# Attention turns of a decoder layer: query transposes moved beside the probability transposes

## The chip, the cores and the metric

The kernel runs on one core of one Trainium2 chip. The metric is the device time of one execution in microseconds (us); the number given for a kernel is the median of its runs. Five engines work side by side, each through its own queue in order: PE (TensorE, matrix products and transposes, with its weight loads shown as PEld), DVE (VectorE), ACT (ScalarE), POOL (GpSimd) and SP (SyncE, which issues the DMAs).

## The reference

One layer of a hybrid decoder over 512 tokens and 1024 features, in fp32:

```
h = RMSNorm(x)
[x_rnn | g_rnn | q | k | v | gate_a | gate_b] = h @ w_in
A = (RG-LRU(conv4(x_rnn)) * gelu(g_rnn)) @ w_rnn_proj
B = attention(q, k, v) @ w_attn_proj
x += (sigmoid(gate_a) * A + sigmoid(gate_b) * B) @ w_out
x += relu(RMSNorm(x) @ w_up)^2 @ w_down
x += (p @ w_ple_proj) * sigmoid(RMSNorm(x) @ w_ple_gate)
```

Attention: 16 query heads and 4 key heads of 64, each query head normalised and rotated (rotary embedding), a sliding window of 128 tokens, and a sink per head that joins the softmax's maximum and its sum. The query block of 128 tokens sees its own block of keys and the one before; the first block sees its own alone.

## The kernel before, in words

Weights come in 143 units of 128x1024. Each is loaded, and split by ACT (`wh`, L118) and DVE (`wl`, L119) into two parts, so that a product is three fp32r matmuls (L145 to L147). PE works through the layer: k and v, then q (L258), attention mixed with the products for `gate_b` and `gate_a` ("gates"), the recurrent branch, the output product, the MLP and the last gate.

The attention stage is the loop at L601: eight turns, u = 0 to 7, where turn u handles query block n = u mod 4 for eight of the heads (u < 4 the first eight). A turn has two halves, g = 0 and 1, of four heads each. A half computes the scores on PE (`scores`, tile `S`, one PSUM buffer), masks and copies them and takes the maximum (`softmax_max`: for n > 0 ACT copies to `sm`, L456, DVE merges the other block under a mask, L457, reduces, L464, and makes four small 128x4 tiles, L465 to L468; for n = 0 DVE alone, L459), takes exponentials on ACT (`softmax_exp`, four at L474 and one at L477), and divides by the sum (`softmax_norm`: DVE L482 and L483, then four POOL operations, L486; in the last half of turn 7 DVE does those four). The probabilities are transposed on PE (`p_transpose`, tile `ppt`, L494) and go out of PSUM on DVE twice, each under a mask (`p_evac`, L505; for n = 0 once on ACT, L503). `pv` (L516, tile `po`) multiplies them with v, and `o_split` (L524 on ACT, L525 on DVE) stores the result. Each half also contains one gate product of 24 matmuls (`proj` on p0 or p1), with its evacuation on DVE (`gate_evac`, L596).

The transposes of half 1 of turn u-1 stand in turn u, behind p0 and ahead of the scores of half 1; those of half 0 stand at the end of their own turn. Queries of the next turn are prepared inside a turn: `q_rope` (four DVE operations, L405 to L408, from `q_raw` to the tile `ra`), `q_transpose` (four PE transposes, L417, tile `pqt`; two ACT copies, L423, and two DVE subtractions, L425, to the tiles `qt`), and, two turns ahead, `q_scale` (ACT L386, DVE L388 and L390, POOL L392).

The order of PE, ACT, SP and POOL is the order of the program text (`manual_schedule`, L68). DVE's order is not: a scheduler sets it when the program is built, by its own costs, and it is fixed from then on. A DVE instruction that waits therefore holds whatever the scheduler has put behind it. PSUM: `ppt` and `pqt` share two `tr` buffers, `pgate` and `po` four `mm` buffers; `qt` has four buffers, two turns' worth.

Of the kernel before, what the change touches and what calls it, by code (L numbers as in the profile page):

```python
# [9 lines left out]
F32 = mybir.dt.float32  # L10
F32R = mybir.dt.float32r
AF = mybir.ActivationFunctionType
ALU = mybir.AluOpType
# [57 lines left out]
def layer_kernel(ctx, tc, w_all, x_t, p_t, vecs, row, ctab, out_t):  # L71
    nc = tc.nc
# [32 lines left out]
    def wissue(parts=1):  # L105
        u = order.pop(0)
        ready[u] = wsplit(u, wp, W_BUFS, parts)
# [15 lines left out]
    def wload(u):  # L123

        while u not in ready or (order and len(ready) <= AHEAD):
            wissue()
        return ready.pop(u)
# [110 lines left out]
    def s_ps(name):  # L238
        return ps.tile([P, 4, 256], F32, tag="S", name=name, bufs=1)

    def s_banks(name):
        wide = s_ps(name).rearrange("p a b -> p (a b)")
        return [wide[:, 0:S], wide[:, S : 2 * S]]
# [151 lines left out]
    def q_rope(u):  # L395
        n = u % NB
        src = q_raw.pop(u).rearrange("p (h d) -> p h d", d=HD)
        a = ftile(f"ra_{u}").rearrange("p (h d) -> p h d", d=HD)
        b = ftile(f"rb_{u}").rearrange("p (h d) -> p h d", d=HD)
        tt = nc.vector.tensor_tensor  # L400

        def tb(t, lo, hi):
            return t[:, n, lo:hi].unsqueeze(1).broadcast_to([P, 8, hi - lo])

        tt(out=a, in0=src, in1=tb(ccq, 0, HD), op=ALU.mult)  # L405
        tt(out=b[:, :, 0:32], in0=src[:, :, 32:64], in1=tb(ssq, 0, 32), op=ALU.mult)
        tt(out=b[:, :, 32:64], in0=src[:, :, 0:32], in1=tb(ssq, 32, 64), op=ALU.mult)
        tt(out=a, in0=a, in1=b, op=ALU.add)  # L408
        q_rot[u] = a

    def q_transpose(u, pt=None):


        a = q_rot.pop(u)
        pt = tr_ps(f"pqt{u}") if pt is None else pt
        for i in range(4):
            nc.tensor.transpose(pt[:, i * P : (i + 1) * P],  # L417
                                a[:, 2 * i : 2 * i + 2, :].rearrange("p a d -> p (a d)"), ident)
        qt = [att.tile([P, 4, P], F32R, tag="qt", name=f"qt{u}{j}", bufs=4) for j in range(2)]
        rows = [slice(0, HD), slice(HD, P)]  # L420
        src = [pt[own].rearrange("p (i t) -> p i t", t=P) for own in rows]
        for j, own in enumerate(rows):
            nc.scalar.activation(qt[j][own], src[j], AF.Copy)  # L423
        for j, own in enumerate(rows):
            nc.vector.tensor_tensor(out=qt[j][rows[1 - j]], in0=src[j],  # L425
                                    in1=qt[j][own].bitcast(F32), op=ALU.subtract)
        q_t[u] = qt

    def window(u):
        n = u % NB  # L430
        return max(n - 1, 0), (2 if n else 1)
# [39 lines left out]
    def softmax_exp(u, g):  # L471
        sm, st = probs[u, g]
        for i in range(4):
            nc.scalar.activation(sm[:, i, :], sm[:, i, :], AF.Exp, bias=st[:, 1, i : i + 1],  # L474
                                 scale=q_sc[u][:, 4 * g + i : 4 * g + i + 1],
                                 accum_out=st[:, 2, i : i + 1])
        nc.scalar.activation(st[:, 3], st[:, 3], AF.Exp)  # L477
# [19 lines left out]
    def p_evac(u, g):  # L497
        pt = p_t_.pop((u, g))
        n = window(u)[1]
        for kb in range(n):  # L500
            prt = ftile(f"pt{u}{g}{kb}")
            if n == 1:
                nc.scalar.activation(prt, pt, AF.Copy)  # L503
            else:
                nc.vector.tensor_tensor(out=prt.rearrange("p (i t) -> p i t", t=P),  # L505
                                        in0=pt.rearrange("p (i t) -> p i t", t=P),
                                        in1=heads4(keep[kb]), op=ALU.mult)
            p_t_[u, g, kb] = prt
# [67 lines left out]
    def q_first():  # L576
# [5 lines left out]
    qkv_group(2, q_banks, [  # L582
        lambda: (k_transpose(norm["rot"]), q_first()),
        k_double,
        lambda: q_transpose(0, s_banks("pqt0")[0]),
    ])
    rb = norm["x"]
    q_evac(1, q_banks)
# [10 lines left out]
    fills = [U_GB + m for m in range(KC)] + [U_GA + m for m in range(KC)]  # L599

    for u in range(8):  # L601
        w0 = wload(fills[len(gates)])
        p0 = mm_ps(f"pgate_{u}_0")
        s0 = scores(u, 0)
        softmax_max(u, 0, s0)
        proj(p0, w0, xg)
        if u:
            p_transpose(u - 1, 1)
            p_evac(u - 1, 1)
        softmax_exp(u, 0)  # L610
        if u < 7:
            q_rope(u + 1)
        softmax_norm(u, 0)
        if u < 6:
            q_scale(u + 2)
        gate_evac(p0, f"gate_{u}_0")
        s1 = scores(u, 1)
        if u:
            o_split(u - 1, pv(u - 1))
        softmax_max(u, 1, s1)  # L620
        w1 = ready.pop(fills[len(gates)])
        p1 = mm_ps(f"pgate_{u}_1")
        proj(p1, w1, xg, range(0, CUT))
        if u < 7:
            q_transpose(u + 1)
        wissue()
        softmax_exp(u, 1)
        softmax_norm(u, 1)
        proj(p1, w1, xg, range(CUT, KC))
        gate_evac(p1, f"gate_{u}_1")  # L630
        p_transpose(u, 0)
        p_evac(u, 0)
# [347 lines left out]
```

## Time and profile before

| | us |
|---|---|
| median of 3 runs (lowest, highest) | 837.55 (837.51, 838.27) |
| the profiled execution | 837.6 |
| its span, first to last instruction | 835.5 |
| PE busy in the span | 829.4 (99%) |
| DVE, ACT, POOL busy | 522.1 (62%), 365.0 (44%), 101.4 (12%) |
| attention stage, turns 1 to 7 (first scores of turn 1 to the first matmul of the recurrent branch) | about 87 to 200 |

The profile is one execution; about 2.1 us of its 837.6 lie outside the span. A row of a timeline gives start, duration, engine, line, operation, tiles written and read, shape and count; several equal neighbours are merged into one row, with the time from the first's start to the last's end. In brackets stands the idle time of the engine before the row and what ended it. PE starts a matmul before the one ahead of it has ended, so the distance between starts is its price, not the duration; DVE and ACT overlap neighbours by about 0.1 us.

### The profile page before, as it was taken

The numbers are of one execution on the slowest core, as the hardware profiler recorded it, in microseconds if no ns is written. First come the engines' busy times: TensorE is split into PE (matmuls) and PEld (weight loads), VectorE is DVE, ScalarE is ACT, GpSimd is POOL, SyncE is SP. The second block draws the span as 40 slices with busy tenths as digits, with TensorE's granted clock in tenths as the row PEclk, the third lists the DMA queues.
The fourth block names the chain that finished last, engine by engine and source line by source line (L and its number), as shares of the span: only waits on it lengthen the run. The fifth ranks groups of instructions, "written<-read, shape, count | busy, mean of one in ns | idle before, by whom it ended". The sixth has DMA issues, their size and how long they took to land.

```text
span 835.5 us, 9915 instructions
## 1 busy us (share of the span) xinstructions
PE 829.4 (99%) x3780; PEld 678.9 (81%) x3780; DVE 522.1 (62%) x768; ACT 365.0 (44%) x581; POOL 101.4 (12%) x123
## 2 busy tenths in 40 slices
PE   9999999999999999999999999999999999999997
PEld 7888877877888888888888888888888888888886
DVE  4687798886766878486567533653355435655563
ACT  7434665663578895633343221231222212333430
POOL 2922432421011110000210000000000000012100
PEclk9999999999999999999999999999999999999999
DMA  7344122122232232235333322223223232233141
GB/s 251 126 115 138 51 80 72 51 77 76 76 100 76 76 102 100 76 127 186 131 103 109 104 98 102 89 89 119 86 97 100 101 102 76 100 102 101 51 163 39
DMA packets 25744, 84.00 MB, mean 101 GB/s; under 512 B 3040, under 2 KB 3424, under 8 KB 25696
## 3 DMA queue, kind: packets, MB, share of 16 engines
q1 hardware_dynamic: 25552, 83.32, 30.0%
q8 instruction: 30, 0.49, 0.2%
q14 instruction: 18, 0.15, 0.1%
q10 hardware_dynamic: 144, 0.05, 0.0%
HBM read 80.20 MB, written 2.10 MB: 99 GB/s over the span
## 4 chain that ended last, share of the span: by engine, by line
PE 99%; DMA 0%; DVE 0%; ACT 0%; issue 0%
PE pu L145 7%; PE pd L145 7%; PE pd L147 7%; PE pu L147 7%; PE pd L146 7%; PE pu L146 7%; PE pq L258 5%; PE pgate L145 4%; PE pgate L147 4%; PE pgate L146 4%; PE pkv L258 3%; PE pyb L145 2%; PE S L441 2%; PE px L145 2%; PE pgl L145 2%; PE pyb L146 2%
## 5 line engine op out<-in xcount | busy, mean ns | idle before, releaser
L119 DVE TENSOR_TENSOR wl<-wr,wh 128x1024 fp32r<-128x1024 f32 (+1 forms) x144 | 180.6, 1257 | 56.1 <-ACT wh L118 56.1
L118 ACT ACTIVATE wh<-wr 128x1024 fp32r<-128x1024 f32 (+1 forms) x144 | 149.7, 1045 | 130.5 <-PE pd L146 98.5
L146 PE MATMUL pu<-x1g,wh 128*128 128x512 f32 x256 | 99.6, 389 | 0.0
L145 PE MATMUL pu<-x1g,wh 128*128 128x512 f32 x256 | 99.6, 389 | 0.0
L147 PE MATMUL pu<-x1g,wl 128*128 128x512 f32 x256 | 99.6, 389 | 0.0
L145 PE MATMUL pd<-u,wh 128*128 128x512 f32 x256 | 99.6, 389 | 0.0
L146 PE MATMUL pd<-u,wh 128*128 128x512 f32 x256 | 99.6, 389 | 0.0
L147 PE MATMUL pd<-u,wl 128*128 128x512 f32 x256 | 99.6, 389 | 0.0
L131 ACT ACTIVATE u<-up 128x512 fp32r<-128x512 f32 x32 | 20.2, 633 | 124.4 <-DVE up L847 124.4
L213 POOL TENSOR_TENSOR sq<-sq,sq_x 128x512 f32<-128x512 f32 x14 | 18.2, 1298 | 453.5 <-ACT sq_x L211 453.5
L856 DVE TENSOR_TENSOR xr<-pd,xr 128x512 f32<-128x512 f32 x32 | 22.1, 692 | 81.5 <-PE pd L147 81.5
L147 PEld LDWEIGHTS pu<-x1g,wl 128*128 128x128 f32 x256 | 48.0, 188 | 10.1
L147 PEld LDWEIGHTS pd<-u,wl 128*128 128x128 f32 x256 | 48.0, 188 | 10.0
L146 PEld LDWEIGHTS pd<-u,wh 128*128 128x128 f32 x256 | 48.0, 188 | 10.0
L146 PEld LDWEIGHTS pu<-x1g,wh 128*128 128x128 f32 x256 | 48.1, 188 | 10.0
L145 PEld LDWEIGHTS pd<-u,wh 128*128 128x128 f32 x256 | 48.0, 188 | 9.9
L145 PEld LDWEIGHTS pu<-x1g,wh 128*128 128x128 f32 x256 | 48.0, 188 | 9.9
L145 PE MATMUL pgate<-xg,wh 128*128 128x512 f32 x128 | 51.4, 402 | 0.0
L147 PE MATMUL pgate<-xg,wl 128*128 128x512 f32 x128 | 50.2, 392 | 0.0
L146 PE MATMUL pgate<-xg,wh 128*128 128x512 f32 x128 | 50.0, 391 | 0.0
L846 DVE TENSOR_TENSOR up<-pu,rb_x 128x512 f32<-128x512 f32 x32 | 22.0, 691 | 40.2 <-PE pu L147 40.1
L474 ACT ACTIVATE sm<-sm,st,sc 128x128 f32<-128x128 f32 x64 | 30.8, 483 | 23.6 <-DVE st L468 21.6
(225 smaller groups left out, 1620.1 us busy)
## 6 DMA issues: line engine op xcount, KB each, us to landing
wr<-in_w_all SPq DMA_DIRECT2D x142, 512.0 KB, 3.3
x<-in_x_t SPq DMA_DIRECT2D x8, 256.0 KB, 5.6
xr<-in_x_t SPq DMA_DIRECT2D x8, 256.0 KB, 3.6
out<-pgt SPq DMA_DIRECT2D x7, 256.0 KB, 2.1
kt<-kt SPq DMA_DIRECT2D x8, 128.0 KB, 2.2
wr<-in_w_all SPq DMA_DIRECT2D x2, 256.0 KB, 3.6
pk<-in_p_t SPq DMA_DIRECT2D x2, 256.0 KB, 3.8
tab<-in_ctab SPq DMA_DIRECT2D x1, 384.0 KB, 6.8
```

What stands on the lines that cost most here:

```text
L118: nc.scalar.activation(wh[:, c], raw[:, c], AF.Copy)
L119: nc.vector.tensor_tensor(out=wl[:, c], in0=raw[:, c], in1=wh[:, c].bitcast(F32), op=ALU.subtract)
L131: nc.scalar.activation(r[:, 0, :], src, AF.Copy)
L145: nc.tensor.matmul(out, ah, bh, start=start, stop=False)
L146: nc.tensor.matmul(out, ah, bl, start=False, stop=False)
L147: nc.tensor.matmul(out, al, bh, start=False, stop=stop)
L213: nc.gpsimd.tensor_tensor(out=acc, in0=acc, in1=t, op=ALU.add)
L258: nc.tensor.matmul(banks[n], a[:, part, n * P : (n + 1) * P], w[:, c], start=k == 0 and i == 0, stop=k == KC - 1 and i == 2)
L441: nc.tensor.matmul(pss[:, i, :], q_t[u][i % 2][:, 2 * g + i // 2, :], kt[part][:, kv, b0 * P : b0 * P + 256], start=part == 0, stop=part == 1)
L474: nc.scalar.activation(sm[:, i, :], sm[:, i, :], AF.Exp, bias=st[:, 1, i : i + 1], scale=q_sc[u][:, 4 * g + i : 4 * g + i + 1], accum_out= ...
L846: nc.vector.tensor_tensor(out=y, in0=pu, in1=r1, op=ALU.mult)
L856: nc.vector.tensor_tensor(out=x1[m], in0=pd, in1=x1[m], op=ALU.add)
```

## The change

In turns 1 to 6 the rotation of the next turn's queries (`q_rope(u + 1)`) is written at the top of the turn instead of behind the exponentials of half 0. Their four transposes stand right behind those of the probabilities, ahead of the scores of half 1, instead of in the middle of p1. The evacuation of the transposed queries becomes a function of its own that is called behind the exponentials of half 0. Turn 0 keeps its order.

```
--- before.py
+++ after.py
@@ -419,12 +419,15 @@
         qt = [att.tile([P, 4, P], F32R, tag="qt", name=f"qt{u}{j}", bufs=4) for j in range(2)]
         rows = [slice(0, HD), slice(HD, P)]
         src = [pt[own].rearrange("p (i t) -> p i t", t=P) for own in rows]
-        for j, own in enumerate(rows):
-            nc.scalar.activation(qt[j][own], src[j], AF.Copy)
-        for j, own in enumerate(rows):
-            nc.vector.tensor_tensor(out=qt[j][rows[1 - j]], in0=src[j],
-                                    in1=qt[j][own].bitcast(F32), op=ALU.subtract)
         q_t[u] = qt
+
+        def evac():
+            for j, own in enumerate(rows):
+                nc.scalar.activation(qt[j][own], src[j], AF.Copy)
+            for j, own in enumerate(rows):
+                nc.vector.tensor_tensor(out=qt[j][rows[1 - j]], in0=src[j],
+                                        in1=qt[j][own].bitcast(F32), op=ALU.subtract)
+        return evac
 
     def window(u):
         n = u % NB
@@ -582,7 +585,7 @@
     qkv_group(2, q_banks, [
         lambda: (k_transpose(norm["rot"]), q_first()),
         k_double,
-        lambda: q_transpose(0, s_banks("pqt0")[0]),
+        lambda: q_transpose(0, s_banks("pqt0")[0])(),
     ])
     rb = norm["x"]
     q_evac(1, q_banks)
@@ -599,6 +602,8 @@
     fills = [U_GB + m for m in range(KC)] + [U_GA + m for m in range(KC)]
 
     for u in range(8):
+        if 0 < u < 7:
+            q_rope(u + 1)
         w0 = wload(fills[len(gates)])
         p0 = mm_ps(f"pgate_{u}_0")
         s0 = scores(u, 0)
@@ -607,9 +612,12 @@
         if u:
             p_transpose(u - 1, 1)
             p_evac(u - 1, 1)
+        qt_evac = q_transpose(u + 1) if 0 < u < 7 else None
         softmax_exp(u, 0)
-        if u < 7:
-            q_rope(u + 1)
+        if qt_evac:
+            qt_evac()
+        if u == 0:
+            q_rope(1)
         softmax_norm(u, 0)
         if u < 6:
             q_scale(u + 2)
@@ -621,8 +629,8 @@
         w1 = ready.pop(fills[len(gates)])
         p1 = mm_ps(f"pgate_{u}_1")
         proj(p1, w1, xg, range(0, CUT))
-        if u < 7:
-            q_transpose(u + 1)
+        if u == 0:
+            q_transpose(1)()
         wissue()
         softmax_exp(u, 1)
         softmax_norm(u, 1)
```

What the program's order is before and now, at three places of turn 3 (which prepares the queries of turn 4). Names: `ppt21` are the transposed probabilities of turn 2, half 1; `sm30`, `st30` the scores and statistics of turn 3, half 0; `pt210`, `pt211` the two masked copies of `ppt21`; `qt40`, `qt41` the transposed queries of turn 4. Lines of the changed kernel are 3 higher at this place (L505 is L508).

DVE at the head of turn 3, before:

```order
L457 COPY_PREDICATED sm30_1216<-tab_72,S30_1207 128x512
L464 TENSOR_REDUCE st30_1219<-sm30_1216 128x4
L465 TENSOR_TENSOR st30_1219<-st30_1219,sc_3_935 128x4
L466 TENSOR_TENSOR st30_1219<-st30_1219,rowb_73 128x4
L467 TENSOR_SCALAR st30_1219<-st30_1219 128x4
L468 TENSOR_TENSOR st30_1219<-rowb_73,st30_1219 128x4
L505 TENSOR_TENSOR pt210_1254<-ppt21_1249,tab_72 128x512
L505 TENSOR_TENSOR pt211_1256<-ppt21_1249,tab_72 128x512
```

and now:

```order
L460 COPY_PREDICATED sm30_1222<-tab_72,S30_1213 128x512
L508 TENSOR_TENSOR pt210_1260<-ppt21_1255,tab_72 128x512
L467 TENSOR_REDUCE st30_1225<-sm30_1222 128x4
L508 TENSOR_TENSOR pt211_1262<-ppt21_1255,tab_72 128x512
L468 TENSOR_TENSOR st30_1225<-st30_1225,sc_3_946 128x4
L469 TENSOR_TENSOR st30_1225<-st30_1225,rowb_73 128x4
L470 TENSOR_SCALAR st30_1225<-st30_1225 128x4
L471 TENSOR_TENSOR st30_1225<-rowb_73,st30_1225 128x4
```

The first evacuation of `ppt21` has moved from behind the maximum of half 0 to ahead of its reduction, and the second into it. (The `q_rope` that was right behind these rows now stands ahead of them, in front of the division of turn 2, half 1.)

DVE in the middle of turn 3, from the half-1 mask to the half-1 maximum, now (before, the row of `pt300` came three rows behind L468 of `st31`, and the two rows of `qt` stood between the rows of `st31`):

```order
L428 TENSOR_TENSOR qt40_1269<-pqt4_1264,qt40_1269 64x512
L428 TENSOR_TENSOR qt41_1270<-pqt4_1264,qt41_1270 64x512
L388 TENSOR_REDUCE sc_5_1288<-asq_5_1286 128x8
L528 TENSOR_TENSOR o0_706<-po2_1303,o0_706 128x4x128
L390 TENSOR_SCALAR sc_5_1288<-sc_5_1288,e64_180 128x8
L460 COPY_PREDICATED sm31_1310<-tab_72,S31_1294 128x512
L119 TENSOR_TENSOR wl31_1334<-wr31_1332,wh31_1333 128x1024
L467 TENSOR_REDUCE st31_1313<-sm31_1310 128x4
L599 TENSOR_TENSOR gate_3_1_1361<-pgate_3_1_1319,rb_x_402 128x512
L468 TENSOR_TENSOR st31_1313<-st31_1313,sc_3_946 128x4
L508 TENSOR_TENSOR pt300_1368<-ppt30_1363,tab_72 128x512
L469 TENSOR_TENSOR st31_1313<-st31_1313,rowb_73 128x4
```

The `qt` rows have moved ahead of the half-1 mask, and a weight split, a gate evacuation and the evacuation of `ppt30` have moved into the half-1 maximum.

ACT in turn 3, from the exponentials of half 0 to the copy of the half-1 scores, now (before, the two `qt` rows came last):

```order
L477 ACTIVATE sm30_1222,st30_1225<-sm30_1222,st30_1225,sc_3_946 128x128 x4
L480 ACTIVATE st30_1225<-st30_1225 128x4
L426 ACTIVATE qt40_1269<-pqt4_1264 64x512
L426 ACTIVATE qt41_1270<-pqt4_1264 64x512
L386 ACTIVATE asq_5_1286<-q11_700 128x512
L527 ACTIVATE o0_706<-po2_1303 128x4x128
L459 ACTIVATE sm31_1310<-S31_1294 128x512
```

The two copies to `qt` have moved ahead of the square, the output split and the copy of the half-1 scores. POOL's and SP's orders are unchanged.

## Rows read from the trace of the kernel before

**Rows 1.** The page, part 4: chain of work that ended last, by engine

```profile
PE 99%; DMA 0%; DVE 0%; ACT 0%; issue 0%
```

**Rows 2.** Windows, a full turn and turn 7: stretch, us, busy by engine, clock, DMA

```profile
119.16:135.42 16.26, 16.26 (x88) 12.64 (x86) 14.73 (x33) 9.63 (x26) 5.25 (x9) 1.00 0.19 66
...
183.85:199.61 15.76, 15.76 (x83) 12.24 (x82) 12.00 (x27) 8.53 (x27) 3.86 (x8) 1.00 0.28 85
```

**Rows 3.** Timeline of PE: transposes of half 1, turns 1, 2, 3, 5, 6, 7

```profile
108.95 0.81 PE L494 MATMUL ppt<-ident,sm 128*128 128x128 f32 x4
...
125.68 0.60 PE L494 MATMUL ppt<-ident,sm 128*128 128x128 f32 x4
...
141.89 0.60 PE L494 MATMUL ppt<-ident,sm 128*128 128x128 f32 x4
...
173.51 0.60 PE L494 MATMUL ppt<-ident,sm 128*128 128x128 f32 x4
...
190.37 0.60 PE L494 MATMUL ppt<-ident,sm 128*128 128x128 f32 x4
...
203.15 0.63 PE L494 MATMUL ppt<-ident,sm 128*128 128x128 f32 x4
```

**Rows 4.** Timeline of PE: products with v in turns 2, 3 and 6

```profile
110.63 2.17 PE L516 MATMUL po<-pt,kv 128*64 128x512 f32 x8
...
127.12 1.94 PE L516 MATMUL po<-pt,kv 128*64 128x512 f32 x8
...
174.99 2.49 PE L516 MATMUL po<-pt,kv 128*64 128x512 f32 x8
```

**Rows 5.** Timeline of ACT: starts of exponentials, and what follows them

```profile
94.66 0.48 ACT L474 ACTIVATE sm<-sm,st,sc 128x128 f32<-128x128 f32 x1
...
125.83 0.49 ACT L474 ACTIVATE sm<-sm,st,sc 128x128 f32<-128x128 f32 x1 [2.70 <-DVE st L468]
...
127.85 0.61 ACT L386 ACTIVATE asq<-q 128x512 f32<-128x512 f32 x1
...
132.54 1.21 ACT L423 ACTIVATE qt<-pqt 64x512 fp32r<-64x512 f32 x2 [2.33 <-PE pqt L417]
...
135.69 0.49 ACT L474 ACTIVATE sm<-sm,st,sc 128x128 f32<-128x128 f32 x1 [0.85 <-DVE st L468]
...
159.36 0.48 ACT L474 ACTIVATE sm<-sm,st,sc 128x128 f32<-128x128 f32 x1
```

**Rows 6.** Timeline of DVE: turns 1 to 3

```profile
85.39 1.41 DVE L425 TENSOR_TENSOR qt<-pqt,qt 64x512 fp32r<-64x512 f32 x2 [1.07 <-ACT qt L423]
...
122.44 0.17 DVE L483 RECIPROCAL st<-st 128x4 f32<-128x4 f32 x1
122.53 1.23 DVE L119 TENSOR_TENSOR wl<-wr,wh 128x1024 fp32r<-128x1024 f32 x1
123.67 0.73 DVE L457 COPY_PREDICATED sm<-tab,S 128x512 f32<-128x512 int32 x1
124.44 0.69 DVE L464 TENSOR_REDUCE st<-sm 128x4 f32<-128x512 f32 x1
...
126.31 1.29 DVE L505 TENSOR_TENSOR pt<-ppt,tab 128x512 f32<-128x512 f32 x2 [0.52 <-PE ppt L494]
127.52 0.68 DVE L405 TENSOR_TENSOR ra<-q,cc_q 128x512 f32<-128x512 f32 x1
...
138.03 0.15 DVE L482 TENSOR_TENSOR st<-st 128x4 f32<-128x4 f32 x1
```

**Rows 7.** Timeline of POOL: divisions of half 1 and, the middle row, of half 0

```profile
106.91 2.46 POOL L486 TENSOR_SCALAR sm<-sm,st 128x128 f32<-128x128 f32 x4 [5.57 <-ACT wh L118]
...
114.48 1.41 POOL L486 TENSOR_SCALAR sm<-sm,st 128x128 f32<-128x128 f32 x4 [5.11 <-DVE sc L390]
...
122.81 2.23 POOL L486 TENSOR_SCALAR sm<-sm,st 128x128 f32<-128x128 f32 x4 [5.30 <-DVE st L483]
```

**Rows 8.** Windows, the end of the kernel, behind PE's last matmul (columns as above)

```profile
833.00:835.50 2.50, 0.00 (x0) 0.00 (x0) 0.00 (x0) 0.00 (x0) 0.00 (x0) 0.71 0.17 58
```

More of the change, by code (lines that the diff above doesn't have):

```diff
@@ L421, in q_transpose, with evac @@
         src = [pt[own].rearrange("p (i t) -> p i t", t=P) for own in rows]
[L422 to L426, printed above, removed]
-        q_t[u] = qt
+        q_t[u] = qt
+        def evac():
+            for j, own in enumerate(rows):
+                nc.scalar.activation(qt[j][own], src[j], AF.Copy)
+            for j, own in enumerate(rows):
+                nc.vector.tensor_tensor(out=qt[j][rows[1 - j]], in0=src[j],
+                                        in1=qt[j][own].bitcast(F32), op=ALU.subtract)
+        return evac
     def window(u):
@@ L584, in layer_kernel @@
         k_double,
-        lambda: q_transpose(0, s_banks("pqt0")[0]),
+        lambda: q_transpose(0, s_banks("pqt0")[0])(),
     ])
@@ L601, in layer_kernel @@
     for u in range(8):
+        if 0 < u < 7:
+            q_rope(u + 1)
         w0 = wload(fills[len(gates)])
@@ L609, in layer_kernel @@
             p_evac(u - 1, 1)
+        qt_evac = q_transpose(u + 1) if 0 < u < 7 else None
         softmax_exp(u, 0)
-        if u < 7:
-            q_rope(u + 1)
+        if qt_evac:
+            qt_evac()
+        if u == 0:
+            q_rope(1)
         softmax_norm(u, 0)
@@ L623, in layer_kernel @@
         proj(p1, w1, xg, range(0, CUT))
-        if u < 7:
-            q_transpose(u + 1)
+        if u == 0:
+            q_transpose(1)()
         wissue()
```

## The prediction, made before the changed kernel was run

> **What bounds the kernel now.** I read the chain of waits on the page first: PE holds 99% of it [rows 1], so the time is PE's own work, and a change counts only if it shortens that work or makes PE wait. Then the timeline of PE through the attention stage, since the change is there. The reader is to look at the transposes of half-1 probabilities (`ppt`), which need the division of the turn before: four of them last 0.60 us when nothing holds them [rows 3]. I name them by the half they finish, though they stand one turn later: `ppt11` (turn 1, half 1) at 108.95, `ppt21` at 125.68, `ppt31` at 141.89, `ppt51` at 173.51, `ppt61` at 190.37, `ppt71` at 203.15. By their durations `ppt11` was late by 0.21, `ppt71` by 0.03, the others not. The products with v show the same kind of small loss: 2.17 and 2.49 in turns 2 and 6 against 1.94 in turn 3 [rows 4], 0.23 and 0.55 us. All that PE loses here in the kernel before is about 1.0 us. Last I read ACT, DVE and POOL for the path from one `ppt` to the next, because it has little slack: in turn 2 the division on POOL runs from 122.81 to 125.04 and `ppt21` starts at 125.68 [rows 3, 7].
>
> **What it removes from PE.** A full turn takes 16.26 us, turn 7 without query transposes 15.76 [rows 2]: a run of four transposes in the middle of a product costs 0.50. Four more behind a run of four cost at most 0.60, their whole duration [rows 3], and at least 0.35, if the last one's tail is as long as a start of two; I take 0.45, near the upper row, a quarter off for the overlap. The gain is 0.05 a turn (-0.10 to 0.15), six times: 0.3 us where PE sets the pace. No matmul is added or removed.
>
> **What it adds: a longer path on DVE and ACT.** The rows of the order show it. Before, DVE made the maximum of half 0 ahead of the evacuation of `ppt` and ACT's exponentials began at 125.83, while DVE's evacuation waited 0.52 for `ppt21` until 126.31 [rows 5, 6]. Now the first evacuation stands ahead of the reduction. It waits for PE, PE's `ppt` waits for POOL, and the maximum of half 0 is queued behind it on DVE. That closes a loop: evacuation of `ppt21`, maximum and exponentials of turn 3 half 0, its `qt` copies, half 1, division, `ppt31`, and again. Its length, with the durations of the rows:
>
> From the first evacuation to the exponentials of half 0: reduction to exponentials takes 1.39 alone (124.44 to 125.83), two evacuations 1.21 (126.31 to 127.52) [rows 5, 6], together 2.60. From there to the mask of half 1 (L457): exponentials 2.02 (125.83 to 127.85), `qt` copies on ACT 1.21, the `qt` pair on DVE 1.41, which needs both copies, then a reduction and a split at 0.60 each (half of the 1.21) and a small one, 0.1 [rows 5, 6]: 5.94. ACT's copy of the half-1 scores, at 0.6 an operation behind the `qt` copies, is done before that, so DVE sets it. From the mask to the exponentials of half 1: the mask 0.65 (0.73 less overlap), a weight split 1.14 (122.53 to 123.67), reduction and gate evacuation 0.60 each, two evacuations of `ppt30` 1.21 [rows 6], and 0.4 for the four small ones (0.7 alone, 1.39 less 0.69; the others fill their pauses): 4.6. Exponentials to division: 2.34 (135.69 to 138.03) [rows 5, 6]; the moved `q_rope`, two operations at 0.60 and two of half the size, some 2.0, lies beside this and costs nothing, and would cost those 2.0 only if it stood behind the division. The division: 0.2 for L482, 0.37 from L483 to POOL, and 2.23 to 2.46 on POOL, I take 2.35 [rows 6, 7]. Last transpose and hand-offs: POOL ended at 109.37 and `ppt11` at 109.76, and the evacuation starts 0.03 behind [rows 3, 6, 7]: 0.42. The sum is 2.60 + 5.94 + 4.6 + 2.34 + 0.57 + 2.35 + 0.42 = 18.8 us.
>
> PE's own distance from one such `ppt` to the next is 16.2 (125.68 to 141.89) [rows 3]. The loop is longer, so in each turn that it runs through PE waits for the difference.
>
> **Turn by turn.** `ppt11`: turn 1's first exponentials, at 94.66 [rows 5], wait for an ACT evacuation and are not moved. 94.66 + 5.94 + 4.6 + 2.34 + 0.57 + 2.35 + 0.39 = 110.85, against an end of 109.76: +1.1. `ppt21`: 18.8 against 16.3 (16.52 from end to end, less the 0.23 of the v product): +2.5. `ppt31`: +2.6, and a mask and a reduction of turn 4 now stand in `q_rope` and between L482 and L483, one of them uncovered, 0.6 to 0.8: +3.3. `ppt41`: turn 4 has no earlier block, DVE masks straight from PSUM, and the loop is about 13.5 (2.6, exponentials 2.0, `qt` 1.2, three ACT operations 2.1, and 5.7 from exponentials to the end): no wait, and PE leads again. `ppt51` is like `ppt11`, 64.70 later (159.36) [rows 5]: 175.55 against 174.11, +1.4. `ppt61`: no `q_scale`, 0.7 less, but a gate evacuation in the first piece, 0.6 more: 18.7 against 16.3 (16.86 less 0.55): +2.4. `ppt71`: no queries, division on DVE, whose four 128x128 operations, not in the rows, I put at 0.25 (between 0.15 for 128x4 and 0.68 for 128x512 [rows 6]): 3.2 (2.60 and a gate evacuation) + 3.2 (exponentials, then the output split on ACT and DVE at 0.6 each) + 4.1 (4.6 less the second evacuation, now behind the maximum) + 2.34 + 0.4 + 1.0 + 0.4 = 14.6 against 12.8: +1.8. Together +12.5.
>
> From this go the losses that were there: 0.23 and 0.55 in the v products (the evacuation now follows its transposes at once), and 0.1 of the shorter PE work, since four of six turns are set by the loop. That is 11.6. I take 11, since the small DVE steps are added with little overlap: 837.6 + 11 = 848.6. The profiled execution and the median, 837.55, are the same for this purpose. Behind attention PE sets the pace, so what is lost stays lost.
>
> Nothing else is paid. SP's and POOL's queues are unchanged; the `tr` buffers come in the same order, `ppt` and `pqt` in turn; `qt` has two turns of buffers. Weight splits come up to 3 us later, but units are split three ahead.
>
> **Rivals.** First, not slower: the loop is hidden and the transposes pay. PE would lose neither 0.21 nor 0.78 and would gain 0.3: 836.3. For it: PE alone is on the chain [rows 1]. Against it: it needs the loop under 16.2, that is 2.6 off my sum, more than the whole division on POOL. It decides at `ppt21`: if POOL ends ahead of PE there, this is the case. Second, a short division: half 0's takes 1.41 against 2.23 and 2.46 [rows 7], and the long ones ran beside a weight split, which starts 0.1 behind L483 [rows 6]. If ACT's half of the split comes so late that DVE's starts behind the division, five turns save 0.94 each: 843.9. Against it: the late ACT half ends about 3.1 behind the start of the exponentials, POOL starts 2.9 behind it, so they still meet. The Trainium skill (GPSIMD Engine Reference, Key points) names this: POOL shares its SBUF interfaces with VectorE and contends with DVE instructions that read two SBUF inputs, as the split does; the pair of 1.41 and 2.46 agrees. Third, the delay doesn't add up, and only `ppt11`, `ppt51` and `ppt71` are late: 1.1 + 1.4 + 1.8 less 0.8 gives 841.1; DVE would have to make up 2.6 a turn, and its idle rows in these turns are no more than 1.5 (14.73 busy of 16.26) [rows 2]. Fourth, the clock. Behind its last matmul PE stands idle and the mean granted clock of the last 2.5 us is 0.71 [rows 8], a mix of the 2.4 and 1.2 GHz levels. If a wait of 2.5 us did that, the 24 matmuls of p1 would take 5.5 us more, and three turns would be PE's again at 16.2 + 5.5, 2.9 above the loop: 848.6 + 8.7 = 857.3. Against it: the waits come in pieces, a transpose between them. [...]
>
> **How the numbers follow.** Forecast 0.68, not slower 0.06, short division 0.14, no adding up 0.08, clock 0.04. The range takes in the second rival, falls short of the third, and above holds 0.3 to 0.6 more per turn for unseen hand-offs: 842.5 to 852.5. About 0.2%, 1.7 us, is what a measurement of this kernel can tell from none. 836.3 lies within it, so faster gets 0.03, same 0.05, slower 0.92.
>
> **What would show it.** Right: waits of PE for POOL (L486) at `ppt` in turns 2, 3, 4, 6, 7, the largest at `ppt31`, none at `ppt41`; full turns of 18.5 to 19.5 us; PE's wait absent from the rest. The v products at 1.94. Exponentials of half 0 starting about 2.5 behind `ppt`. Wrong: no wait of PE at `ppt21`, DVE idle ahead of its L485 for over 1 us in turns 2 and 3, POOL ending ahead of PE, or a granted clock below 1.00 behind a wait.

## The result, and the profile after

The changed kernel takes 849.75 us (median of 4 runs, 848.27 to 850.43), the kernel before 837.91 us beside it: a ratio of 1.014, 95% interval 1.0127 to 1.0152, so 11.8 us slower. The forecast was 848.6 us in a range of 842.5 to 852.5. The profiled execution has a span of 846.2 us against 835.5, 10.7 more. It is the shortest of the four (848.27 us, mean granted clock 0.999); the others took 849.67 to 850.43 at 0.997 to 0.998, so about 1.1 of the 11.8 does not stand in the rows below. All line numbers of the new kernel are three higher from the query transposes on (L497 is `ppt`, L489 POOL's division, L508 the evacuation of `ppt`).

PE held 99% of the chain of waits on the page [rows 1]; now other engines stand in it:

```profile
PE 87%; DVE 6%; ACT 4%; issue 1%; POOL 1%; DMA 0%; POOLq 0%; ACTq 0%
```

PE's transposes of the half-1 probabilities, from the timeline of PE (start us, us, what; in brackets the idle time ahead and what ended it), are `ppt11`, `ppt21`, `ppt31`, `ppt41`, `ppt51`, `ppt61`, `ppt71`; they answer to [rows 3]:

```profile
109.97 1.38 PE L497 MATMUL ppt<-ident,sm 128*128 128x128 f32 x4 [0.80 <-POOL sm L489]
...
129.04 1.03 PE L497 MATMUL ppt<-ident,sm 128*128 128x128 f32 x3 [1.06 <-POOL sm L489]
...
147.85 1.38 PE L497 MATMUL ppt<-ident,sm 128*128 128x128 f32 x4 [1.65 <-POOL sm L489]
...
164.80 0.60 PE L497 MATMUL ppt<-ident,sm 128*128 128x128 f32 x4
...
181.17 1.02 PE L497 MATMUL ppt<-ident,sm 128*128 128x128 f32 x3 [0.78 <-POOL sm L489]
...
199.51 1.03 PE L497 MATMUL ppt<-ident,sm 128*128 128x128 f32 x3 [1.05 <-POOL sm L489]
...
213.87 0.82 PE L497 MATMUL ppt<-ident,sm 128*128 128x128 f32 x4 [0.70 <-DVE sm L489]
```

The reader is to look at two things. The bracket is only the wait ahead of the first transpose shown; 1.38 in place of 0.60 is waiting too, since each of the four then goes at the pace of POOL's division of its 128x128 block. So the delay is read from the ends: 111.35, 130.07, 149.23, 182.19, 200.54 and 214.69 against 109.76, 126.28, 142.49, 174.11, 190.97 and 203.78 [rows 3]. PE is 1.6, 3.8, 6.7, 8.1, 9.6 and 10.9 late there: the delay grows at each but `ppt41` (165.40 against 158.77, 6.6), which has no wait. Behind it nothing is added: 10.9 there, 10.7 at the end of the span.

The chain of waits in the stretch 109 to 131 us (start, us, what; PE's rows from one `ppt` to the next left out) shows what `ppt21` waited for:

```profile
111.39 0.69 DVE pt L508
112.08 0.59 DVE st L467
112.67 0.60 DVE pt L508
...
113.83 0.27 ACT sm L477
...
115.95 0.49 ACT qt L426
116.45 0.60 ACT qt L426
117.08 0.68 DVE qt L428
117.78 0.69 DVE qt L428
118.50 0.69 DVE sc L388
...
120.05 0.64 DVE sm L460
120.69 1.11 DVE wl L119
121.80 0.60 DVE st L467
122.39 0.60 DVE gate L599
...
124.50 0.29 ACT sm L477
...
126.65 0.17 DVE st L485
126.85 0.19 DVE st L486
...
127.22 1.77 POOL sm L489 x2
129.04 0.33 PE ppt L497
```

This is the loop that the prediction wrote down, and from the first row to the next evacuation, at 130.11, it lasts 18.72 us. PE was on it for 1.07 us only. The two `qt` copies and the DVE pair (L426, L428) stand in its first half, the weight split (L119) and the gate evacuation (L599) inside the maximum of half 1. Windows of the full turn (stretch, us, busy by engine, clock, DMA) say the same from the other side, PE busy 17.3 of 18.68 where it was 16.26 of 16.26 [rows 2]:

```profile
120.84:139.52 18.68, 17.32 (x84) 12.82 (x85) 14.71 (x34) 9.41 (x26) 5.48 (x10) 1.00 0.18 57
```

The granted clock is 1.00 there. The products with v in turns 2 and 3 take 1.94, where turn 2 had 2.17 [rows 4], and POOL's division of half 1 takes 2.47 and 2.46, where it took 2.46 and 2.23 [rows 7]:

```profile
112.66 1.94 PE L519 MATMUL po<-pt,kv 128*64 128x512 f32 x8
...
131.38 1.94 PE L519 MATMUL po<-pt,kv 128*64 128x512 f32 x8
```

```profile
108.50 2.47 POOL L489 TENSOR_SCALAR sm<-sm,st 128x128 f32<-128x128 f32 x4 [5.72 <-ACT wh L118]
...
127.22 2.46 POOL L489 TENSOR_SCALAR sm<-sm,st 128x128 f32<-128x128 f32 x4 [5.44 <-DVE st L486]
```

### The profile page after: what moved, and what is told of

It is laid out like the page before. It is cut to its first block, busy times and chain, and to the rows that moved or that the text cites. A ratio compares the mean times of both kernels' runs of the same rounds, so it can differ in the third digit from the quotient of the medians.

```text
span 846.2 us, 9914 instructions
## 1 busy us (share of the span) xinstructions
PE 833.5 (99%) x3780; PEld 679.0 (80%) x3780; DVE 520.9 (62%) x768; ACT 364.2 (43%) x581; POOL 104.3 (12%) x123
## 4 chain that ended last, share of the span: by engine, by line
PE 87%; DVE 6%; ACT 4%; issue 1%; POOL 1%; DMA 0%; POOLq 0%; ACTq 0%
PE pu L146 7%; PE pu L145 7%; PE pd L145 7%; PE pd L146 7%; PE pd L147 7%; PE pu L147 7%; PE pq L258 5%; PE pkv L258 3%; ACT sm L477 2%; PE pyb L145 2%; PE pgl L145 2%; PE ppg L145 2%; PE ppg L147 2%; PE pyb L146 2%; PE pgl L146 2%; PE pgl L147 2%
## 5 line engine op out<-in xcount | busy, mean ns | idle before, releaser
L119 DVE TENSOR_TENSOR wl<-wr,wh 128x1024 fp32r<-128x1024 f32 (+1 forms) x144 | 181.1, 1260 | 54.6 <-ACT wh L118 54.5
L145 PEld LDWEIGHTS pu<-x1g,wh 128*128 128x128 f32 x256 | 48.0, 188 | 10.1
```

The lines of the kernel that those rows point to most:

```text
L119: nc.vector.tensor_tensor(out=wl[:, c], in0=raw[:, c], in1=wh[:, c].bitcast(F32), op=ALU.subtract)
L145: nc.tensor.matmul(out, ah, bh, start=start, stop=False)
```

## The experiments

The theory: two things together make the loop. DVE, which works in order, has the evacuation of `ppt` ahead of the reduction of half 0, so that the exponentials of half 0 are tied to `ppt`, which waits for the division of the turn before (below: the tie). And the `qt` copies and the pair, now early, lengthen the way from there to the next division. Rivals: the transposes' new place on PE, the rotation at the top, POOL's long division, or a fixed price on PE. One thing limits all these runs: DVE's row is planned anew for each program, so an edit can move more than it names. Ratios are to the kernel before, with 95% intervals; 1.010 is 8.4 us.

**The copies late again.** The transposes stay early.

```diff
         softmax_exp(u, 0)
-        if qt_evac:
-            qt_evac()
...
         proj(p1, w1, xg, range(0, CUT))
+        if qt_evac:
+            qt_evac()
```

> The changed kernel with one thing put back: the two ACT copies to qt and the DVE pair behind them are called where the query transposes stood before, behind the first half of the second gate product. The transposes themselves stay beside ppt, and q_rope stays at the top. Theory (the loop of evacuation, maximum, exponentials, qt copies, half 1, division is longer than PE's 16.2 us, and the qt copies are what made it so): between exponentials and mask of half 1 the copies' 1.20 on ACT and the pair's 1.39 are gone, the pair comes back in part behind the mask, where ACT's copies end 0.6 after it. From the rows of the changed kernel: 1.84 (evacuation to exponentials, since the reduction now stands ahead) + 9.0 to 9.1 (exponentials to exponentials) + 2.15 + 0.57 + 2.3 + 0.42 = 16.4 a turn against PE's 16.2, so at most 0.3 in three turns: 838.5 us, 837 to 840. Rival 1, the transposes' place on PE costs by itself (two runs of fp32 transposes in the middle of the product): stays at 849 to 850. Rival 2, the moved rotation is the price: also 849 to 850. Rival 3, copies and rotation share it: 843 to 846.

Measured: 839.45 us, 1.0024 (1.0014 to 1.0033). Ten of the twelve are back though the transposes are where the change put them, which ends the rival on PE and that on a price of the rotation alone. The edit did more than move the copies: in the new plan the reduction of half 0 stands ahead of the evacuation of `ppt` (turn 3: reduction at 126.87, evacuation at 127.82), only its four small operations behind it, and the evacuation of the half-0 transposes lies behind the maximum of half 1, not in it. Some 1.8 is left, and the rows show it at `ppt`, at POOL's pace:

```profile
109.56 1.10 PE L497 MATMUL ppt<-ident,sm 128*128 128x128 f32 x4
...
126.41 1.38 PE L497 MATMUL ppt<-ident,sm 128*128 128x128 f32 x4
...
144.09 1.02 PE L497 MATMUL ppt<-ident,sm 128*128 128x128 f32 x3 [0.45 <-POOL sm L489]
```

**The tie taken away, with the copies early and late.** An issue rule on DVE, nothing else; `last_max` holds the last small operation of each maximum.

```diff
...
-            p_evac(u - 1, 1)
+            with tc.issue_after(last_max[u, 0].ins):
+                p_evac(u - 1, 1)
```

> The changed kernel with one rule added to DVE's row: the two evacuations of ppt (half 1 of the turn before) are issued behind the last small operation of the maximum of half 0, in every turn. Nothing else is changed by hand; DVE's row is otherwise as in the changed kernel. So the maximum no longer waits for PE's ppt, which waits for POOL. Theory A (two things together: the evacuation ahead of the reduction ties the exponentials of half 0 to ppt, and the qt copies lengthen the way from there): the tie is gone, what is left is DVE's own row: exponentials of half 1 to mask of half 0 4.25 (124.50 to 128.75), mask 0.63, reduction 0.60, small ones 0.7, exponentials to exponentials 10.68 (132.55 to 143.23): 16.9 a turn against PE's 16.2. ppt11 and ppt51, the first of a block, keep 1.59 and 1.34; 0.7 each at ppt21, ppt31, ppt61, 0.9 at ppt71: 6.1, less 0.8 of the v products: 843 us, 841.5 to 844.5. Theory B, the qt copies alone are the price: no change, 849 to 850. Theory C, the order alone is the price: 837.5 to 839.

> The changed kernel with the qt copies and the pair put back behind the first half of the second gate product (839.5 us as measured) and the rule that the evacuation of ppt is issued behind the maximum of half 0. Theory: one small operation of the maximum stood behind the evacuation there, so 1.84 from ppt to the exponentials; without it they start by DVE's row alone, and PE's 16.2 sets the pace in most turns; what is left is POOL's division beside rotation and split. 838.3 us, 837.3 to 839.3. Rival, the 1.8 are the price of the transposes' new place on PE: 839 to 840.

Measured: 843.14 us, 1.0061 (1.0048 to 1.0074), with the copies early; 837.54 us, 0.9999 (0.9990 to 1.0008), with the copies late. The first fell on theory A and between B and C. DVE's rows of it show why it isn't zero; the reduction no longer waits for PE, but it waits its turn behind the split:

```profile
125.00 0.18 DVE L487 RECIPROCAL st<-st 128x4 f32<-128x4 f32 x1
125.75 1.23 DVE L119 TENSOR_TENSOR wl<-wr,wh 128x1024 fp32r<-128x1024 f32 x1 [0.57 <-ACT wh L118]
126.90 0.73 DVE L461 COPY_PREDICATED sm<-tab,S 128x512 f32<-128x512 int32 x1
127.66 0.69 DVE L468 TENSOR_REDUCE st<-sm 128x4 f32<-128x512 f32 x1
```

Over the kernel before, the four are: copies early with the tie 11.8, copies early without it 5.6, copies late with it (the looser tie described above) 1.8, copies late without it 0.0. The 6.3 of the rule with the copies early has only the tie in it, since DVE's row is otherwise the same in turns 2 and 3; with the copies late the rule moved some rows of half 1 too, and the 10.1 between the first and the third holds the copies and what the plan moved with them. The parts don't add (5.6 + 1.8 = 7.4): copies that come early cost 5.6 by themselves, and more where the tie carries each turn's delay into the next.

**The rotation at the top alone, and with the rule.**

```diff
     for u in range(8):
+        if 0 < u < 7:
+            q_rope(u + 1)
...
-        if u < 7:
+        if u == 0:
             q_rope(u + 1)
```

> The kernel before with one part of the change alone: q_rope of turns 2 to 7 is written at the top of the turn; transposes and qt copies stay behind the first half of the second gate product. Theory: the rotation's 2.0 us lie beside ACT's exponentials of half 1, and the evacuation ahead of the reduction delays the exponentials of half 0 to 1.9 to 2.4 behind ppt, but half 1's path then hangs on PE's transposes of the queries, whose copies to the exponentials of half 1 took 9.41 us behind ppt: 9.41 + 2.15 + 0.57 + 2.35 + 0.42 = 14.9 under PE's 16.2. So 837.5 to 839. Rival, the rotation at the top is the price of the change: 847 to 850, with PE waiting for POOL's division at ppt.

> The kernel before with the rotation at the top of the turn (which alone lost 4.9 us) and the rule that the evacuation of ppt is issued behind the maximum of half 0. In DVE's row the weight split and the gate evacuation then also lie behind the maximum of half 1. Theory: it was not the rotation's 2.0 us that cost 4.9 but the row in which the moved rotation left the rest (evacuation ahead of the reduction, split and gate evacuation inside the maximum of half 1): all of it comes back, 838 us, 837 to 839. Rival, the rotation's own time at the top is the price: 842 to 843.

Measured: 842.61 us, 1.0059 (1.0045 to 1.0072), and with the rule 841.42 us, 1.0044 (1.0031 to 1.0058). Both expectations missed: the rotation at the top is not free in the kernel before. With the rule, the timelines of POOL and DVE of that run show what became of it. The rotation (L405 and on) and a weight split now stand beside POOL's division, and it takes 3.81, where half 0's, with neither beside it, takes 1.41:

```profile
114.73 1.41 POOL L487 TENSOR_SCALAR sm<-sm,st 128x128 f32<-128x128 f32 x4 [4.49 <-DVE st L484]
...
122.74 3.81 POOL L487 TENSOR_SCALAR sm<-sm,st 128x128 f32<-128x128 f32 x4 [4.99 <-DVE st L484]
```

```profile
122.38 0.17 DVE L484 RECIPROCAL st<-st 128x4 f32<-128x4 f32 x1
...
123.04 0.68 DVE L405 TENSOR_TENSOR ra<-q,cc_q 128x512 f32<-128x512 f32 x1
...
124.41 1.21 DVE L119 TENSOR_TENSOR wl<-wr,wh 128x1024 fp32r<-128x1024 f32 x1
```

And the evacuation behind the maximum makes the product with v late (128.16, 2.78 in place of 1.94). In the changed kernel the rotation ends at 126.5, ahead of the division at 127.22, and POOL's 2.46 are those of before. So I count the 4.9 and 3.8 as no part of the change's 11.8. Nor is the top dear by itself: in the run above that lost 0.0 the rotation stands there too.

**The rotation away from the top in the changed kernel**, at its old place but for the turn after the next.

```diff
-        src = q_raw.pop(u).rearrange("p (h d) -> p h d", d=HD)
+        src = q_raw[u].rearrange("p (h d) -> p h d", d=HD)
...
-        if 0 < u < 7:
-            q_rope(u + 1)
...
         if u == 0:
             q_rope(1)
+        if u < 6:
+            q_rope(u + 2)
```

> The changed kernel with the rotation taken away from the top of the turn: q_rope is written where it stood before, behind the exponentials of half 0, but for the turn after the next, so that the transposes still find it ready. Transposes and qt copies are as in the changed kernel. Theory: at the top the rotation's 2.0 us lie under ACT's exponentials of half 1 and cost nothing; at the old place one 128x512 and one 128x256 operation of it now stand between the small ones behind the reduction, ahead of the exponentials of half 0: 0.60 + 0.34 = 0.94 more in the loop, at ppt21, ppt31, ppt61, perhaps less 0.3 to 0.5 each for a division on POOL without the rotation beside it: 1.4 to 2.8 more, 851.5 us, 850.5 to 853. Rival, the rotation's move to the top is a part of the price (the run with the rotation alone at the top lost 4.9): 844 to 848.

Measured: 852.28 us, 1.0174 (1.0160 to 1.0188): dearer, as the theory had it. From the evacuation at 131.14 to the exponentials of half 0 at 134.28 are 3.14 there, 2.44 in the changed kernel.

**Cutting the evacuation in two**: ACT's copies early, only the DVE pair late.

```diff
-        def evac():
+        def copies():
             for j, own in enumerate(rows):
                 nc.scalar.activation(qt[j][own], src[j], AF.Copy)
+
+        def pair():
             for j, own in enumerate(rows):
...
-        return evac
+        return copies, pair
...
         softmax_exp(u, 0)
         if qt_evac:
-            qt_evac()
+            qt_evac[0]()
...
         proj(p1, w1, xg, range(0, CUT))
+        if qt_evac:
+            qt_evac[1]()
...
```

> The changed kernel with the evacuation cut in two: ACT's copies to qt stay early, behind the exponentials of half 0, and only the DVE pair is called where it stood before; in DVE's row it then stands behind the mask of half 1, one on each side of the reduction. Theory (the sum of what DVE does one after the other between two evacuations sets the turn): the pair is moved, not removed. Ahead of the mask of half 1 the 1.42 go, but the mask then waits for the o split behind ACT's two copies and lies about 0.75 earlier only; behind the mask the pair comes back and two evacuations of ppt go out, 4.6 to 4.7 in place of 4.55. So 0.65 a turn, at ppt11, ppt21, ppt31, ppt51, ppt61, together 3.3: 846.5 us, 845.5 to 847.5. Rival 1, the pair's 1.39 on DVE is the price: 5 x 1.4 = 7 back, 842.8. Rival 2, ACT's copies are the price and the pair costs nothing: no change, 849.5 to 850.

Measured: 848.90 us, 1.0130 (1.0116 to 1.0144), 0.9 below the changed kernel where 3.3 were expected: a miss, and even the 0.9 is not the loop's. All four executions had a mean granted clock of 1.000, those of the changed kernel 0.997 to 0.999, and the profiled one took 848.74 us, that of the changed kernel 848.27. The loop became longer, 19.05 (evacuations at 111.49 and 130.54) in place of 18.72. The mask came 0.87 earlier behind the exponentials (5.26 in place of 6.13), but from the mask to the exponentials it was 5.20 in place of 4.54, since the pair stands there at 0.71 each; POOL's division started 0.2 later and took 2.77, with the last of the rotation and the split beside it. What is moved within DVE's row is not removed.

**The division on DVE**, in the changed kernel and with the copies late.

```diff
-            eng = nc.vector if (u, g) == (7, 1) else nc.gpsimd
+            eng = nc.vector if u and g == 1 else nc.gpsimd
```

> The changed kernel with the divisions of half 1 in turns 1 to 6 on DVE (as turn 7 has it) in place of POOL. They take about 1.0 us there in place of 2.3 to 2.46 and save a hand-off of 0.37. Theory (one loop through DVE, in order): the first delays of a block shrink by 1.4 (ppt11, ppt51), but in the turns between, DVE has the division itself in its row ahead of the weight split and the mask of half 0, so the next evacuation starts only 0.3 earlier than now: 18.4 a turn in place of 18.7. Sum 2 x 1.4 + 3 x 0.3 = 3.7 at most back: 846 to 847.5, and PE still waits at ppt. Rival, POOL's long division beside the weight split is the whole price and the rest of the path is idle time: 5 x 1.5 to 1.9 back, 840 to 842.5, no waits of PE left at ppt21 and ppt31.

> The changed kernel with the qt copies and the pair put back behind the first half of the second gate product, and with the division of half 1 on DVE. With the copies alone put back 839.5 us were measured, 1.8 over the kernel before, and PE's transposes ppt went at POOL's pace (1.10, 1.38, 1.74 in place of 0.60) while POOL's divisions took 2.46 to 2.97. Theory 1, this rest is POOL's division beside DVE's rotation and split: on DVE it takes 0.8, PE finds it done, 837.5 to 838. Theory 2, the loop goes through DVE's row: the division's 0.8 stand ahead of split and mask of half 0, the evacuation follows the mask at once and comes no earlier: 839 to 840.5, with PE's waits at the scores or the v product in place of ppt.

Measured: 846.22 us, 1.0100 (1.0086 to 1.0114), and 840.41 us, 1.0030 (1.0019 to 1.0041), both as the theory of one row had it: a division 1.6 shorter gives back 3.3 of 11.8, and where the copies are late it costs 0.7. The rows of the first show the end of the division, and the evacuation right behind the mask:

```profile
126.89 0.87 DVE L489 TENSOR_SCALAR sm<-sm,st 128x128 f32<-128x128 f32 x4
127.68 1.22 DVE L119 TENSOR_TENSOR wl<-wr,wh 128x1024 fp32r<-128x1024 f32 x1
128.81 0.72 DVE L460 COPY_PREDICATED sm<-tab,S 128x512 f32<-128x512 int32 x1
129.42 0.68 DVE L508 TENSOR_TENSOR pt<-ppt,tab 128x512 f32<-128x512 f32 x1
```

One thing in it I had not named: part of PE's waiting went to the scores (waits in the stretch 84 to 225: line, for whom, us in all, times, longest). There is one buffer for scores, and the mask of half 1 is what releases it, so the same late mask holds PE a second way:

```profile
PE S L444 <- DVE sm L460: 3.8, 4, 1.4
...
PE ppt L497 <- DVE sm L489: 2.3, 2, 1.6
```

**Work of a known size added**: two exponentials of half 1 done twice, in the changed kernel, in the kernel before, and there with the issue rule. `spare` is a tile that nothing reads, and `st` has a fifth row for its sums.

```diff
...
+        for i in range(2 if u and g else 0):
+            nc.scalar.activation(spare, sm[:, i, :], AF.Exp, bias=st[:, 1, i : i + 1],
+                                 scale=q_sc[u][:, 4 * g + i : 4 * g + i + 1],
+                                 accum_out=st[:, 4, i : i + 1])
...
```

> The changed kernel with work added in a known size: in half 1 of turns 1 to 7 ACT does the first two exponentials twice, the extra ones into a spare tile (0.48 us each, 0.48 from start to start with the read of the sum), 0.96 us ahead of the division. DVE's order is the same but in turn 4. Theory: every turn that goes by the loop gets longer by those 0.96: ppt11, ppt21, ppt31, ppt51, ppt61, ppt71, 6 x 0.96 = 5.8, ppt41 has slack: 855.5 us (854.5 to 856). Rival, the time of the change is a fixed price on PE (switches, clock) and ACT has slack as before (it is idle 4.7 us ahead of these exponentials): 849.5 to 851.

> The kernel before with the same added work as the run with two extra exponentials in half 1 of turns 1 to 7 (0.96 us ahead of each division; there it cost the changed kernel 7.2 us). Theory: the kernel before has slack. By the rows, end of POOL's division plus 0.39 against the end of ppt: ppt21 125.43 against 126.28, 0.85 of slack, ppt31 141.68 against 142.49, 0.81, ppt61 189.39 against 190.97, 1.6, ppt11, ppt51 and ppt71 none. So 3 x 0.96 + 0.11 + 0.15 = 3.1, less up to 0.78 of waits of the v products that it can take the place of: 840.4 us, 839.5 to 841.5. Rival, the added work costs the same wherever it is put (PE's clock, a fixed price): 844.5 to 845.

> The kernel before with the two extra exponentials in half 1 (measured 854.7 us, 16.7 over the kernel before, where 3 were expected; there DVE's row had the evacuation ahead of the reduction in turns 2 and 3) and the rule that the evacuation of ppt is issued behind the maximum of half 0. Weight split and gate evacuation stay inside the maximum of half 1. Theory: the tie to ppt was more than half of the 16.7. What is left: exponentials of half 1 at 9.4 behind ppt, 1.7 for split and gate evacuation, 1.2 for the two extra ones, 2.15 + 0.57 + 2.35 + 0.42 to the end of the next ppt: 17.8 against 16.2, 1.3 to 1.6 in five turns: 845 us, 843 to 847. Rival, the added exponentials themselves (ACT, PE's clock) are the price: 853 to 856.

Measured: 856.95 us, 1.0230 (1.0216 to 1.0244); 854.70 us, 1.0192 (1.0170 to 1.0213); 851.22 us, 1.0161 (1.0145 to 1.0177). The first is 7.2 over the changed kernel where 5.8 were expected. The two take 1.12 (start to start, 105.90 to 107.02) and not 0.96, six times 6.7. Between the profiled executions (848.27 and 856.99 us) the stretch from the first `ppt` (86.88, 87.35) to the end of `ppt71` (214.69, 221.79) grew by 6.6, so the loop did carry the added work, but not evenly: the turn from `ppt21` to `ppt31` took only half of it (19.66 against 19.16), the way from `ppt61` to `ppt71` 1.9 more (16.02 against 14.15), with a lower clock in it, and behind `ppt71` the clock cost 1.75 more. Windows behind `ppt11`, `ppt21`, `ppt31`, `ppt61` and `ppt71` of that run (the last number but two is the granted clock):

```profile
113.00:117.00 4.00, 4.00 (x19) 2.89 (x19) 2.35 (x7) 1.53 (x7) 0.00 (x0) 0.63 0.19 74
...
132.00:136.00 4.00, 3.97 (x19) 2.83 (x20) 2.48 (x8) 0.85 (x3) 0.34 (x1) 0.63 0.38 135
...
152.00:156.00 4.00, 3.98 (x24) 2.39 (x24) 3.43 (x6) 2.11 (x4) 0.00 (x1) 1.00 0.39 131
...
205.00:209.00 4.00, 4.00 (x16) 2.59 (x18) 2.88 (x9) 0.33 (x1) 0.24 (x1) 0.61 0.42 131
...
221.00:225.40 4.40, 4.40 (x15) 3.05 (x15) 2.74 (x6) 0.03 (x1) 0.00 (x0) 0.61 0.35 119
```

The second missed by 14 us. I had counted the slack of the kernel before in the row it had; with the added work the planned row of DVE came out another (evacuation ahead of the reduction in turns 3, 6 and 7 and behind the reduction but ahead of the small operations in turn 2, split and gate evacuation inside the maximum of half 1), and that kernel closed the loop with its copies where they always were. The third takes the tie away and leaves the rest: 3.1 come back, not the 9.7 expected. A part of these medians goes with the clock. In the second run one execution had a mean granted clock of 1.000 and took 850.44 us, the other four 0.992 to 0.996 and 853.74 to 856.73; in the third two had 0.999 and 1.000 and took 849.96 and 849.74, the other two 0.995 and 852.47 and 853.05. By the executions at 0.999 and more the tie is worth 0.5 to 0.7 there, and some 12 over the kernel before stay without it. So in that kernel the tie is the smaller part; how the 12 divide between the added 1.1 a turn and the two operations inside the maximum, I did not settle.

## Why the prediction was right

**The bound and the way of the loss.** PE's chain, the loop as its end, and `ppt` as the place were as forecast: waits for POOL at `ppt11`, `ppt21`, `ppt31`, `ppt51` and `ppt61`, for DVE at `ppt71`, none at `ppt41`, the largest at `ppt31`, full turns of 18.4 to 19.2 from end to end of `ppt`, the v products of turns 2 and 3 at 1.94, no wait behind attention.

**The loop, term by term**, from rows of 111.39 to 130.11. Evacuation to exponentials 2.44 (forecast 2.60). Exponentials to the mask of half 1 6.13 (5.94). Mask to exponentials 4.54 (4.6). Exponentials to division 2.15 (2.34). To POOL 0.57 (0.57). POOL, the last transpose and the hand-offs 2.89 (2.35 + 0.42). Sum 18.72 against 18.8. The mask of half 1 starts at 119.96 by DVE's timeline. Terms that were 0.1 to 0.2 too short (to the mask; POOL and the transpose) and 0.2 too long (to the exponentials of half 0; to the division) cancel, so the sum is nearer than its terms.

**Turn by turn**, as growth of the delay: `ppt11` 1.6 (1.1; 0.2 of the miss is an offset that the run already had in turn 1, whose exponentials start at 94.83, not 94.66), `ppt21` 2.2 (2.5 less 0.23), `ppt31` 3.0 (3.3), `ppt41` -0.1 (0), `ppt51` 1.5 (1.4), `ppt61` 1.5 (2.4 less 0.55), `ppt71` 1.3 (1.8). Sum 10.9 against 11.6, of which the prediction took 11. Three misses are 0.4 to 0.5: `ppt61`, where the loop was 18.35 and not 18.7; `ppt71`, where the way from `ppt61` was 14.15 and not 14.6; and `ppt11`, which was late by the offset, by the mask of half 1 0.2 behind its term, and by a division that POOL started 0.91 behind L485 and not 0.57, less 0.2 in the other terms. The growth is 0.7 under the terms as added, and the 0.6 that the prediction took off for overlap covers it; that allowance was a guess, and that it fitted is luck. The forecast, 848.6, is nearer to the profiled execution, 848.27, than to the median, whose further 1.1 no term of it holds.

**The gain from PE.** At `ppt41` of the changed kernel the four query transposes start 0.44 behind those of the probabilities, and the scores 0.35 behind them, as they stood behind `ppt` before; 0.44 for the forecast's 0.45. Of the whole take, 0.05 a turn, the medians 837.54 (late copies and the rule) and 837.58 show nothing. In the profiled executions the stretch from the first `ppt` to the end of `ppt71` is 116.71 there (87.52 to 204.23) and 117.08 before (86.70 to 203.78), with about as much lost on the way, 1.1 at `ppt11` and `ppt51` against 1.0. One execution of each is little, but the term fits, and is too small to matter.

**The rivals.** Not slower: POOL ended after PE was ready, at `ppt21` by more than 1. A short division: it stayed at 2.46, since the split still met it (DVE's L119 at 127.60, POOL's division 127.22 to 129.68). The Trainium skill (GPSIMD Engine Reference, Key points) says that POOL shares its SBUF interfaces with VectorE and contends with DVE instructions that read two SBUF inputs; the traces agree, with 1.41 beside neither split nor rotation, 2.46 beside a split, 3.81 beside rotation and split. No adding up: it added up, at `ppt21`, `ppt31` and `ppt61` too. The clock: 1.00 in the window shown, and in all of attention (84 to 215) of that execution, so it is not in the rows above. The three longer executions had 0.997 to 0.998 over the run; whether waits in attention cost it there stays open. The run with 1.1 us more ahead of each division met it, so this rival was nearer than its 0.04 says.

**What the prediction missed, though it cost nothing here.** That the one buffer of scores is a second way in which a late mask of half 1 holds PE. That the tie and the copies multiply was in the sum but not said; the four runs showed that the two don't add. And it called the rotation at the top covered as if by its place; it is covered because in this kernel the division comes later than the rotation ends; in the kernel before, with the rotation moved up, it was not.

## What to carry to other kernels

When a change makes work ready earlier, ask where the in-order engine's row puts it, and write the loop through that row as one sum against the bound engine's own turn: here 18.8 against 16.2 gave the time to within 1.2 us. A short operation that waits for the bound engine, placed ahead of the next stage's work, turns slack into a loop; one issue rule that put the maximum first gave back 6.3 us, and late copies, with the row that came of them, 10.1. Of a planner's row, re-read the whole after every edit: in the two runs of the kernel before that lost 4.9 and 16.7 us, an edit elsewhere had rearranged it. And compare medians only with the granted clock of each execution beside them: of one kernel here, the executions at 1.000 and 0.992 lay 6.3 us apart.

## What the runs showed of the hardware

The granted clock fell in the run with two more exponentials: 0.63, 0.63, 0.61 and 0.61 in four windows behind waits at `ppt11`, `ppt21`, `ppt61` and `ppt71`, a mix of the 2.4 and 1.2 GHz levels, and 1.00 behind `ppt31`, where PE had waited in the same pieces as at `ppt21`. No run shows what makes the difference. Matmuls of 128x512 started 0.43 apart there in place of 0.23:

```profile
220.96 0.83 PE L502 MATMUL ppt<-ident,sm 128*128 128x128 f32 x4 [1.71 <-DVE sm L494]
221.55 0.56 PE L145 MATMUL px<-xg,wh 128*128 128x512 f32 x1
221.90 0.63 PE L146 MATMUL px<-xg,wh 128*128 128x512 f32 x1
222.33 0.63 PE L147 MATMUL px<-xg,wl 128*128 128x512 f32 x1
```

From 221.55 to the v product at 225.37 nine of them took 3.82, 1.75 more than nine at 0.23, and no loop hides it behind `ppt71`: it is enough for the 1.4 by which that run was over its expectation, of which the longer exponentials (1.12 for 0.96) explain some too; no run separates the two. In the changed kernel PE waited 1.65 ahead of `ppt31` and kept 1.00 in the window behind it.

```profile
150.00:154.00 4.00, 4.00 (x21) 2.22 (x20) 3.57 (x13) 3.18 (x11) 0.52 (x2) 1.00 0.03 11
```

The Trainium skill (TensorE: Matmul & The Clock Gate, Why this matters for your kernels) warns of idle gaps between bursts of matmuls; this run agrees in so far as each lower window stood behind a wait of PE, with 1.89, 1.05, 1.13 and 1.71 us as the longest at the four `ppt` and transposes in between.

The first exponential of 128x128 of a group of the two extra ones took 0.62 from start to start (105.90, 106.52), the second 0.50, the later ones of the group 0.48; no run shows why.
